# Gate and up projections as Strassen block products, a separate down projection through DRAM, and a merge in 512-column products

## The chip, the cores and the metric

The kernel runs on one core of a Trainium2 chip. The metric is the device time of one execution in microseconds; lower is better. PE below is the matrix engine, DVE, ACT and POOL are the vector, scalar and GpSimd engines, and SP issues most of the DMAs.

## The reference

One layer for a sequence of 1024 rows of width 1024, in float32. The change touches the lines after the two mixers (y_a, y_b), cut here to what matters:

```python
x = x + (g_a * y_a + g_b * y_b) @ w_out            # merge, w_out 1024 x 1024
h = rmsnorm(x, norm_ffn_g)
x = x + (silu(h @ w_ffn_gate) * (h @ w_ffn_up)) @ w_ffn_down   # D_FF = 2816
return rmsnorm(x, norm_final_g)
```

## The kernel before

Every float32 operand is split into a rounded part and the rest (`split`, L156: a cast to the short type `fp32r` on ACT, then a subtraction on DVE), and every product is three products of such parts: high by high, high by low, low by high (`mm3`, L145, products in L152 to L154). So a weight block costs a DMA, a cast `wh` (L161) and a subtraction `wl` (L164) before PE can use it. The class `Weights` (L75) holds a list of all weight blocks in the order of use, loads them into two raw buffers with DMAs of SP (L93) and splits them into three pairs of buffers `wh`, `wl`; `next` gives one block and prepares the ones behind it (`ahead`). Each engine does its instructions in the order in which the program wrote them, so the order of the calls is the order of each queue.

The stages at the end of the program are these. `up_b` (L1136) makes y_b, multiplies it by its gate, adds the other half and writes the merged activations `mhi`, `mlo` (64 groups of three 512-column products, the last `mlo` on POOL). `load_x1` (L1179) brings x into SBUF by four 1 MB DMAs on the ACT queue, in front of the casts of `up_b`. `merge` (L1184) multiplies by w_out: four column groups of 256, two halves of the inner dimension, eight row tiles, four blocks, three products each (L1199 to L1201), 768 products in all; the sum goes onto x1 in SBUF (L1206), the squares are summed on ACT (L1208), `norm` scales rows on DVE and POOL (L204 to L207) and `turn` transposes them on PE and splits them back into `mhi`, `mlo` (L209 to L220). `ffn` (L1259) then goes over 22 column blocks f of 128: `gate_up(f)` (L1265) gives 96 products of 512 columns (for f = 0: 192 of 256, set between the last turns of the merge), Silu on ACT (L1281), a product on DVE (L1285) and a split into `shi`, `slo`; after every second f `down(c)` (L1320) does 96 products of 512 columns (L1331 to L1333) and adds them to x1 in SBUF (L1336). The last `down` also sums squares (L1342), scales rows and stores them (L1347).

Functions that the diff touches, as they were:

## Time and profile before

| what | us |
|---|---|
| median of 3 runs | 1673.09 (1671.81 to 1673.85) |
| the profiled execution: its own time | 1678.37 |
| its span in the trace | 1676.6 |
| PE busy in that span | 1626.2 (97%) |
| DVE, ACT, POOL busy | 857.9, 516.7, 382.1 |

The times are of whole executions. The span is what the trace of one execution covers, from its first to its last instruction; the execution itself took 1.8 us longer. Busy time of PE counts an instruction from its start to its modelled end; consecutive products overlap, so what one product costs is read from the distance of two starts, not from its duration.

### The profile page before, as it was taken

The page shows a single profiled execution, that of the slowest core. Times are in us where ns is not written, and L with a number is a line of the kernel's source. Part 1 is how long each engine was busy: PE and PEld are TensorE (multiplying, and loading weights), DVE is VectorE, ACT ScalarE, POOL GpSimd, SP SyncE. Part 2 cuts the span into 40 slices and gives each one's busy share as a digit, 9 for nine tenths or more (in the row PEclk, how much of TensorE's full clock was granted, in tenths as well). Part 3 has the DMA queues.
Part 4 walks back from the last instruction along what each step waited for, and adds up shares of the span by engine and source line. Part 5 has one row for each costly group of instructions (what it writes and reads, how often), then busy time and mean ns, then how long its engine had stood idle before and what let it go on. Part 6 is the DMA issues. An engine that isn't in the chain of part 4 may idle for free.

```text
span 1676.6 us, 22642 instructions
## 1 busy us (share of the span) xinstructions
PE 1626.2 (97%) x8612; PEld 1385.2 (83%) x8612; DVE 857.9 (51%) x1685; ACT 516.7 (31%) x1136; POOL 382.1 (23%) x438
## 2 busy tenths in 40 slices
PE   8989999999998999998999999999999999999996
PEld 7767888888886899997799988888888888888885
DVE  7268776511325899997923623324324334243245
ACT  5212324312210698996122321111111211211113
POOL 1027676300112455564502300000000000000004
PEclk9999999999999999999999999999999999999999
DMA  6333442374339612102722021111111211111112
GB/s 213 96 105 107 132 128 79 102 182 120 118 100 278 170 42 57 34 27 103 250 63 64 27 62 51 38 50 51 50 38 51 63 38 48 53 50 39 50 38 100
DMA packets 166785, 145.50 MB, mean 87 GB/s; under 512 B 17434, under 2 KB 142774, under 8 KB 166679
## 3 DMA queue, kind: packets, MB, share of 16 engines
q1 hardware_dynamic: 165591, 139.88, 28.2%
q10 hardware_dynamic: 1088, 4.19, 0.6%
q8 instruction: 68, 1.11, 0.3%
q14 instruction: 38, 0.31, 0.1%
HBM read 109.83 MB, written 32.11 MB: 85 GB/s over the span
## 4 chain that ended last, share of the span: by engine, by line
PE 84%; DVE 5%; DMA 4%; ACT 2%; issue 1%; SPq 1%; POOL 1%; POOLq 0%; ACTq 0%; DVEq 0%
PE a L152 16%; PE a L154 16%; PE a L153 16%; PE O L1059 3%; PE T L1041 3%; PE S L943 3%; PE b L1331 2%; PE b L1332 2%; PE b L1333 2%; PE c L1333 2%; PE c L1331 2%; PE c L1332 2%; PE a L1201 2%; PE a L1199 2%; PE a L1200 2%
## 5 line engine op out<-in xcount | busy, mean ns | idle before, releaser
L152 PE MATMUL a<-mhi,wh 128*128 128x512 f32 (+1 forms) x736 | 280.0, 380 | 0.2 <-ACT mhi L219 0.2
L153 PE MATMUL a<-mlo,wh 128*128 128x512 f32 (+1 forms) x736 | 279.6, 380 | 0.3 <-DVE mlo L220 0.3
L154 PE MATMUL a<-mhi,wl 128*128 128x512 f32 (+1 forms) x736 | 279.6, 380 | 0.0
L164 DVE TENSOR_TENSOR wl<-wr,wh 128x1024 fp32r<-128x1024 f32 x108 | 142.0, 1316 | 254.9 <-ACT wh L161 242.0
L152 PE MATMUL a<-hhi,wh 128*128 128x512 f32 x448 | 185.0, 413 | 0.4 <-POOL wh L159 0.4
L154 PE MATMUL a<-hhi,wl 128*128 128x512 f32 x448 | 178.4, 398 | 2.2 <-DVE wl L164 2.2
L153 PE MATMUL a<-hlo,wh 128*128 128x512 f32 x448 | 178.5, 398 | 0.0
L206 POOL TENSOR_SCALAR x<-x,rstd 128x1024 f32<-128x1024 f32 (+1 forms) x4 | 8.2, 2038 | 707.6 <-DVE rstd L186 707.6
L153 PEld LDWEIGHTS a<-mlo,wh 128*128 128x128 f32 x736 | 138.4, 188 | 26.7 <-DVE mlo L220 0.5
L152 PEld LDWEIGHTS a<-mhi,wh 128*128 128x128 f32 x736 | 138.4, 188 | 26.7 <-ACT mhi L219 0.5
L154 PEld LDWEIGHTS a<-mhi,wl 128*128 128x128 f32 x736 | 138.4, 188 | 26.2
L161 ACT CAST wh<-wr 128x1024 fp32r<-128x1024 f32 x76 | 79.3, 1046 | 244.2 <-PE c L1333 173.4
L1014 POOL TENSOR_SCALAR P<-P,sum,gates 128x640 f32<-128x640 f32 (+3 forms) x192 | 125.4, 669 | 115.5 <-DVE sum L1008 64.4
L1043 DVE TENSOR_TENSOR PTl<-T,PTh 128x512 fp32r<-128x512 f32 (+3 forms) x200 | 104.0, 543 | 10.2 <-ACT PTh L1042 8.4
L152 PEld LDWEIGHTS a<-hhi,wh 128*128 128x128 f32 x448 | 85.7, 191 | 25.2 <-issue 6.2
L1336 DVE TENSOR_TENSOR x<-x,b 128x512 f32<-128x512 f32 x88 | 60.5, 687 | 87.3 <-PE b L1333 86.7
L154 PEld LDWEIGHTS a<-hhi,wl 128*128 128x128 f32 x448 | 85.5, 191 | 23.0 <-DVE wl L164 2.6
L153 PEld LDWEIGHTS a<-hlo,wh 128*128 128x128 f32 x448 | 85.9, 192 | 17.7
L994 ACT ACTIVATE P<-P,m 128x640 f32<-128x640 f32 (+7 forms) x128 | 95.8, 748 | 9.2 <-DVE m L978 9.2
L159 POOL TENSOR_SCALAR wh<-wr 128x1024 fp32r<-128x1024 f32 x34 | 36.9, 1085 | 259.4 <-PE a L153 149.8
L1042 ACT CAST PTh<-T 128x512 fp32r<-128x512 f32 (+3 forms) x200 | 88.7, 476 | 21.1 <-PE T L1041 20.4
L1281 ACT ACTIVATE sg<-a 128x512 f32<-128x512 f32 x44 | 26.3, 599 | 218.7 <-PE a L154 218.7
(353 smaller groups left out, 3389.0 us busy)
## 6 DMA issues: line engine op xcount, KB each, us to landing
wr<-in_w_in SPq DMA_DIRECT2D x28, 512.0 KB, 4.9
wr<-in_w_ffn_gate SPq DMA_DIRECT2D x22, 512.0 KB, 3.8
wr<-in_w_ffn_up SPq DMA_DIRECT2D x22, 512.0 KB, 4.0
wr<-in_w_ffn_down SPq DMA_DIRECT2D x22, 512.0 KB, 3.5
gd<-evf SPq DMA_DIRECT2D x32, 256.0 KB, 2.1
Q<-qd SPq DMA_DIRECT2D x64, 128.0 KB, 3.1
xt<-in_x SPq DMA_DIRECT2D x8, 512.0 KB, 5.7
sga<-gd SPq DMA_DIRECT2D x8, 512.0 KB, 5.0
```

Of the source, the lines that this page charges most:

```text
L152: mm(ps, a, c, start=start and k == 0, stop=False, skip_group_check=True)
L153: mm(ps, a, d, start=False, stop=False, skip_group_check=True)
L154: mm(ps, b, c, start=False, stop=stop and k == nk - 1, skip_group_check=True)
L161: nc.scalar.copy(hi, src)
L164: (nc.gpsimd if lo_eng == "pool" else nc.vector).tensor_tensor(lo, src, hi, op=OP.subtract)
L994: AC.activation(p[:, 0:nk], p[:, 0:nk], AF.Exp, bias=m[:, 0:1], scale=-1.0, accum_out=sm(0))
L1014: sc = lambda x, y, z: GP.tensor_scalar(x, x, a[:, y:y + 1], gate(z), op0=OP.mult, op1=OP.mult)
L1042: AC.copy(oh, t[:, 0:len(cc), :])
L1043: V.tensor_tensor(ol, t[:, 0:len(cc), :], oh, op=OP.subtract)
L1331: nc.tensor.matmul(ps, hi[:, t], wh[:, 0, col], start=f == 0, stop=False)
L1332: nc.tensor.matmul(ps, hi[:, t], wl[:, 0, col], start=False, stop=False)
L1333: nc.tensor.matmul(ps, lo[:, t], wh[:, 0, col], start=False, stop=f == 1)
```

## The change

Five things are done.

1. **Merge.** w_out is cut into units of two inner blocks by 512 columns (`unit`), and the products become 512 columns wide: 384 instead of 768. The first four row tiles use 8 units of 24 products; then the tiles 4 and 5, and 6 and 7, use 8 units each of 12 products, so w_out is read three times. x is loaded one tile at a time on the ACT queue (4 buffers `x1`), and after the norm a tile's x is stored to DRAM (`xd`), on the same queue.
2. **Turn.** For the tiles 4 to 7 `turn` also builds the sums of block rows that Strassen's scheme (in Winograd's form) needs, on DVE, POOL and ACT, in tiles with one buffer each, and splits five results.
3. **Gate and up.** 22 matrices (11 pairs of column blocks, gate and up in turn). Each is a 2 by 2 block product done with 7 block products of 12 products (512 columns), 84 in place of 96. The four sums of weight blocks are made on POOL (`sums`), the sums of results on DVE and POOL.
4. **Gated results** go to DRAM, 44 tiles `sd` of 256 KB, stored by SP.
5. **Down** is a phase of its own: 44 steps (two halves h of the rows, 22 f), 24 products each, all sums of a half in the eight PSUM banks; w_ffn_down is read twice, `sd` is read back, and x comes back from `xd` at f = 16. The squares and the scaling of tiles 0 to 3 run in the second half, those of tiles 4 to 7 at the end.

The order of the weight list is cut in two (`until`): w_ffn_down is loaded only from the end of the gate and up phase on. `Bacc` gets `dynamic_dma_scratch_size=1024`. The core of the diff (the removed `load_x1`, `merge` and `ffn` are printed above):

```diff
+    def load(self, n):
+        if n >= len(self.mats):
+            return
+        K, (name, j) = self.K, self.mats[n]
+        ts = []
+        for kh in range(2):
+            t = (K.W.raw if n % 2 else self.raw).tile([P, 4, 256], F32, name="wr", tag="wr")
+            K.nc.sync.dma_start(t, K.A[name][512 * kh:512 * kh + 512, 256 * j:256 * j + 256]
+                                .rearrange("(k p) c -> p k c", p=P))
+            ts.append(t)
...
+    def pair(self, n, a, b, src):
+        W, sh = self.K.W, [P, 2, 4, P]
+        hi, lo = W.hl.tile(sh, FR, name="wh", tag="wh"), W.hl.tile(sh, FR, name="wl", tag="wl")
+        if src is not None and b is not None:
+            self.K.split(hi, lo, src, "act", "dve")
+        else:
+            A = self.r[n]
+            for x, t in enumerate(((1, 1), (1, 2)) if b is not None else ((2, 2),)):
+                self.K.split(hi[:, x], lo[:, x], A(*t), "act", "dve")
...
+        s = self.s[n] = self.pool.tile([P, 4, 4, P], F32, name="S", tag="S", bufs=1)
+        o = lambda i: s[:, i]
+        GP.tensor_tensor(o(1), A(2, 1), A(2, 2), op=OP.add)
+        GP.tensor_tensor(o(0), o(1), A(1, 1), op=OP.subtract)
+        GP.tensor_tensor(o(2), A(1, 1), A(2, 1), op=OP.subtract)
+        GP.tensor_tensor(o(3), A(1, 2), o(0), op=OP.subtract)
...
+    def out(self, n, i, h, t):
+        K, (name, j) = self.K, self.mats[n]
+        if name == "w_ffn_gate":
+            K.nc.scalar.activation(t, t, AF.Silu)
+            self.gates[j, i, h] = t
+        else:
+            K.nc.gpsimd.tensor_tensor(t, t, self.gates.pop((j, i, h)), op=OP.mult)
+            K.nc.sync.dma_start(self.sd[2 * j + i][h], t)
...
+    def early(self):
+        self.sums(0)
+        self.p1(0)
+        self.p1(1)
+        self.p2(0)
+        self.p2(1)
...
+    def rest(self, n, early):
+        K, last = self.K, n + 1 == len(self.mats)
+        V, AC, GP = K.nc.vector, K.nc.scalar, K.nc.gpsimd
+        y = K.bank("b")
+        self.product(n, 6, y)
+        u2 = self.p.pop(n)
+        V.tensor_tensor(u2, u2, y, op=OP.add)
+        if not early:
+            self.p2(n)
+            self.t4(n)
+            self.load(n + 2)
+        z = K.bank("a")
+        self.product(n, 5, z)
+        p5 = self.tile("p5")
+        AC.copy(p5, z)
+        if n:
+            self.t1(n + 1)
+        v = K.bank("b")
+        self.product(n, 7, v)
+        u3 = self.tile("u3")
+        V.tensor_tensor(u3, u2, v, op=OP.add)
+        GP.tensor_tensor(p5, u3, p5, op=OP.add)
+        self.out(n, 1, 1, p5)
+        self.product(n, 3, z, first=False)
+        V.tensor_tensor(u2, u2, z, op=OP.add)
+        self.out(n, 0, 1, u2)
+        if last:
+            self.after()
+        self.t2(n + 1)
+        c = K.bank("c")
+        self.product(n, 4, c)
+        V.tensor_tensor(u3, u3, c, op=OP.add)
+        self.out(n, 1, 0, u3)
+    def run(self, after):
+        self.after = after
+        self.t2(0)
+        for n in range(len(self.mats)):
+            self.t3(n)
+            self.sums(n + 1)
+            if n < 2:
+                self.t4(n)
+                self.load(n + 2)
+            else:
+                self.p1(n)
+            self.rest(n, n < 2)
...
     def up_b(self, pool, m_):
...
-        self.load_x1(x1)
...
+        def load(tt):
+            x1[tt] = pool.tile([P, D], F32, name="x1", tag="x1", bufs=4)
+            nc.scalar.dma_start(x1[tt], self.A["x"][P * tt:P * tt + P, :])
...
+        def norm(tt):
+            xns[tt] = self.norm(pool, x1[tt], g, "xn", "dve", 2)
+            nc.scalar.dma_start(xd[tt], x1.pop(tt))
...
+            v = lambda n: pool.tile([P, 4, P], F32, name=n, tag=n, bufs=1)
+            t1, t2, t3, t4, b22 = (v(n) for n in ("t1", "t2", "t3", "t4", "b22"))
+            V.tensor_tensor(t1, pb, first(0, 0), op=OP.subtract)
+            AC.copy(b22, pc)
+            GP.tensor_tensor(t1, t1, first(1, 0), op=OP.subtract)
+            V.tensor_tensor(t3, b22, pb, op=OP.subtract)
+            GP.tensor_tensor(t2, b22, t1, op=OP.subtract)
+            GP.tensor_tensor(t4, first(0, 1), t2, op=OP.subtract)
+            GP.tensor_tensor(t4, t4, first(1, 1), op=OP.add)
+            for x, hi, lo in ((b22, m[0][:, 4:8, at], m[1][:, 4:8, at]),
+                              (t3, td[1][0][:, :, c], td[1][1][:, :, c]),
+                              (t1, m[0][:, 0:4, at], m[1][:, 0:4, at]),
+                              (t2, td[0][0][:, :, c], td[0][1][:, :, c]),
+                              (t4, td[2][0][:, :, c], td[2][1][:, :, c])):
+                self.split(hi, lo, x, "act", "dve")
+        unit = lambda u, q: self.W.next("w_out", 256 * u, 2, 512 * q, 512, ("act", "dve"))
+        for tt in range(4):
+            load(tt)
+        for q in range(2):
+            banks = [self.bank("a") for _ in range(4)]
+            for u in range(4):
+                w = unit(u, q)
+                for tt in range(4):
+                    part(w, u, tt, banks[tt])
+                    if u == 3:
+                        add(tt, q, banks[tt])
+                        if q and tt < 2:
+                            norm(tt)
+        load(4)
+        load(5)
+        for first in (4, 6):
+            for q in range(2):
+                banks = [self.bank("a") for _ in range(2)]
+                for u in range(4):
+                    w = unit(u, q)
+                    last = first == 6 and q == 1
+                    if last and u >= 2:
+                        if u == 2:
+                            ffn.load(1)
+                        ffn.t1(u - 2)
+                    for i in range(2):
+                        tt = first + i
+                        part(w, u, tt, banks[i])
+                        if u == 3:
+                            add(tt, q, banks[i])
+                            if q:
+                                norm(tt)
+                    if first == 4 and q == 0:
+                        turn(u)
+                        if u < 2:
+                            norm(u + 2)
+                            load(u + 6)
+                    if first == 6 and q == 0 and u % 2:
+                        turn(4 + u // 2)
+                    if first == 6 and q == 0 and u == 0:
+                        ffn.load(0)
+        ffn.early()
+        turn(6)
+        turn(7)
...
+                t = pool.tile([P, 512], F32, name="sr", tag="sr", bufs=4)
+                self.nc.sync.dma_start(t, sd[f][h])
...
+        for n, (h, f) in enumerate(order):
             if f == 0:
+                banks = [[self.bank("a" if tt < 2 else "bc"[c]) for c in range(2)] for tt in range(4)]
+            split(n + 2)
+            load(n + 4)
+            hi, lo = parts[n]
+            wh, wl = self.W.next("w_ffn_down", P * f, 1, 0, D, ("act", "dve"))
+            if f == 16:
+                for tt in range(4 * h, 4 * h + 4):
+                    x1[tt] = pool.tile([P, D], F32, name="x1f", tag="x1f", bufs=8)
+                    nc.sync.dma_start(x1[tt], xd[tt])
...
+                ss, one = (pool.tile([P, k], F32, name=f"ssf{k}", tag=f"ssf{k}", bufs=4) for k in (2, 1))
+                added(4 + tt, banks[tt], ss)
+                V.tensor_reduce(one, ss, axis=mybir.AxisListType.X, op=OP.add)
+                r = self.rstd(pool, one)
+                if tt < 3:
+                    scaled(4 + tt, slice(0, D), r, "pool" if tt == 1 else "dve")
+                else:
+                    scaled(7, slice(512, D), r, "pool")
+                    scaled(7, slice(0, 512), r, "dve")
...
+        def after():
+            W.until(None)
+            W.ahead(2, 4)
+            loads[3](1)
+        ffn.run(after)
+        for p in (ffn.late, fp, rp, tp, mp):
+            p.release()
+        pool = self.pool("dn")
+        self.down(pool, loads, xd)
...
```

The order of the engines' queues changes at three places that matter below. In the rows a name before the arrow is written, those behind it are read; a number behind a name tells buffers of that name apart; "waits" names the engine or the DMA queue that the instruction waits for.

ACT, in the merge between the products of tiles 0 to 3 and those of tiles 4 and 5. Before, at the same place (the last column group), the queue held squares, rstd, turns and casts of weights, and no DMA:

```order
L1208 ACTIVATE scr_8657,ssq0_8653<-x10_8248 128x256 [waits Activation_49]
L178 ACT_TABLE_LOAD
L178 ACTIVATE rstd_9411<-ss2_9409,eps_103 128x2 [waits DVE_49]
L1208 ACTIVATE scr_8657,ssq1_8654<-x11_8249 128x256 [waits DVE_49,Activation_49]
L1208 ACTIVATE scr_8657,ssq1_8654<-x11_8249 128x256 [waits Activation_49]
L178 ACTIVATE rstd_9452<-ss2_9450,eps_103 128x2 [waits DVE_49]
L219 CAST mhi_8246<-b_9512 128x4x128 [waits PE_49]
L219 CAST mhi_8246<-c_9519 128x4x128 [waits PE_49]
L161 CAST wh_9526<-wr_9322 128x1024 [waits DMAHW7_49,Pool_49]
```

Now:

```order
L1385 DMA xd0_8692<-x1_8706 128x1024
L376 ACTIVATE xn_8968,ss_8967<-x1_8708 128x1024 [waits DVE_49]
L360 ACTIVATE rstd_8970<-ss_8967,eps_103 128x1 [waits Activation_49]
L1385 DMA xd1_8693<-x1_8708 128x1024
L1369 DMA x1_8992<-in_x 128x1024 [waits DMAHW1_49]
L1369 DMA x1_8994<-in_x 128x1024 [waits DMAHW2_49,DVE_49]
L343 CAST wh_8998<-wr_8910 128x1024 [waits DMAHW7_49,PE_49]
```

The store of a tile's x, the load of the next tile into the same buffer and the cast of the next unit of w_out now stand one behind the other in ACT's queue.

ACT, at the end of the merge, the turns of the tiles 6 and 7 and what follows. Before, two turns were two casts each, with products of `gate_up(0)` on PE between them:

```order
L219 CAST mhi_8246<-b_9717 128x4x128 [waits PE_49]
L219 CAST mhi_8246<-c_9724 128x4x128 [waits PE_49]
L1281 ACT_TABLE_LOAD
L1281 ACTIVATE sg_9755<-a_9667 128x512 [waits PE_49]
L219 CAST mhi_8246<-b_9757 128x4x128 [waits PE_49]
L219 CAST mhi_8246<-c_9764 128x4x128 [waits PE_49]
```

Now:

```order
L343 CAST T0h_8642<-t2_9575 128x4x128 [waits Pool_49]
L343 CAST T2h_8646<-t4_9577 128x4x128 [waits Pool_49]
L1402 COPY b22_9610<-c_9597 128x512 [waits DVE_49,PE_49]
L343 CAST mhi_8246<-b22_9610 128x4x128 [waits Activation_49]
L343 CAST T1h_8644<-t3_9608 128x4x128 [waits DVE_49]
L343 CAST mhi_8246<-t1_9606 128x4x128 [waits Pool_49]
L343 CAST T0h_8642<-t2_9607 128x4x128 [waits Pool_49]
L343 CAST T2h_8646<-t4_9609 128x4x128 [waits Pool_49]
L343 CAST wh_9635<-S_9500 128x1024
```

The second turn's copy waits for the first turn's last results on DVE, and the cast of the weight sums S that the next product needs stands behind both turns.

SP, at the passage to the down phase. Before, the loads of w_ffn_down stood between those of the next gate and up blocks:

```order
L93 DMA wr_11671<-in_w_ffn_gate 128x8x128 [waits DMAHW5_49,DVE_49]
L93 DMA wr_11705<-in_w_ffn_up 128x8x128 [waits DMAHW6_49,DVE_49]
L93 DMA wr_11739<-in_w_ffn_gate 128x8x128 [waits DMAHW7_49,DVE_49]
L93 DMA wr_11875<-in_w_ffn_up 128x8x128 [waits DMAHW0_49,DVE_49]
L93 DMA wr_11935<-in_w_ffn_down 128x1024 [waits DMAHW1_49,DVE_49]
```

Now:

```order
L235 DMA sd211_8691<-p5_12426 128x512 [waits DMAHW7_49,Pool_49]
L235 DMA sd201_8689<-p1_12378 128x512 [waits DMAHW0_49,Pool_49]
L94 DMA wr_12461<-in_w_ffn_down 128x1024 [waits DMAHW1_49,Activation_49]
L94 DMA wr_12467<-in_w_ffn_down 128x1024 [waits DMAHW2_49,DVE_49]
L94 DMA wr_12473<-in_w_ffn_down 128x1024 [waits DMAHW3_49,DMAHW1_49,DVE_49]
L94 DMA wr_12475<-in_w_ffn_down 128x1024 [waits DMAHW4_49,DMAHW2_49,DVE_49]
L1469 DMA sr_12477<-sd00_8648 128x512 [waits DMAHW5_49]
```

The load of the first gated tile (`sr`) stands behind two stores that wait for POOL and behind two weight loads that wait for a split on DVE.

## Rows read from the trace of the kernel before

**Rows 1.** the page, part 1 (busy time) and the first line of part 4 (the chain)

```profile
PE 1626.2 (97%) x8612; PEld 1385.2 (83%) x8612; DVE 857.9 (51%) x1685; ACT 516.7 (31%) x1136; POOL 382.1 (23%) x438
...
PE 84%; DVE 5%; DMA 4%; ACT 2%; issue 1%; SPq 1%; POOL 1%; POOLq 0%; ACTq 0%; DVEq 0%
```

**Rows 2.** timeline of PE in a gate and up block: start, us, engine, line, output<-inputs

```profile
960.10 0.39 PE L152 MATMUL a<-mhi,wh 128*128 128x512 f32 x1
...
981.18 0.39 PE L152 MATMUL a<-mhi,wh 128*128 128x512 f32 x1
```

**Rows 3.** timeline of PE in a down block

```profile
1002.27 0.39 PE L1331 MATMUL b<-wh,shi 128*128 128x512 f32 x1
...
1008.57 0.40 PE L1331 MATMUL c<-wh,shi 128*128 128x512 f32 x1
```

**Rows 4.** timeline of PE in the merge's first products

```profile
833.52 0.28 PE L1199 MATMUL a<-wh,mhi 128*128 128x256 f32 x1
...
835.92 0.28 PE L1201 MATMUL a<-wh,mlo 128*128 128x256 f32 x1
```

**Rows 5.** timelines of ACT and PE in up_b; in brackets the wait and its releaser

```profile
785.27 4.67 ACTq L1181 DMA_DIRECT2D x<-in_x  x1
...
796.82 1.99 ACT L161 CAST wh<-wr 128x1024 fp32r<-128x1024 f32 x2 [10.53 <-DMA x<-in_x]
...
799.99 0.47 PE L152 MATMUL a<-oh,wh 128*128 128x512 f32 x1 [2.06 <-DVE sgb L1157]
```

**Rows 6.** groups by line and shape, 1050 to 1680 us: busy us, mean ns, waits

```profile
L161 ACT CAST wh<-wr 128x1024 fp32r<-128x1024 f32 x54 | 56.5, 1047 | 156.1 <-PE c L1333 156.1
...
L164 DVE TENSOR_TENSOR wl<-wr,wh 128x1024 fp32r<-128x1024 f32 x54 | 66.1, 1224 | 196.9 <-ACT wh L161 196.9
...
L164 DVE TENSOR_TENSOR slo<-sg,shi 128x512 fp32r<-128x512 f32 x36 | 24.9, 693 | 24.7 <-ACT shi L161 24.7
...
L1342 ACT ACTIVATE scr<-x 128x1024 f32<-128x1024 f32 x6 | 6.4, 1061 | 13.9 <-DVE x L1336 13.7
```

**Rows 7.** groups by line and shape, 780 to 960 us (merge)

```profile
L164 POOL TENSOR_TENSOR mlo<-sgb,mhi 128x512 fp32r<-128x512 f32 x16 | 24.4, 1526 | 30.7 <-DVE mhi L163 16.3 <-issue 14.4
...
L1158 DVE TENSOR_TENSOR sgb<-sgb,pab 128x512 f32<-128x512 f32 x16 | 19.5, 1221 | 0.6
...
L204 DVE SCALAR_TENSOR_TENSOR xn<-x,rstd,gffn 128x1024 f32<-128x1024 f32 x4 | 5.1, 1285 | 0.4
...
L219 ACT CAST mhi<-c 128x512 fp32r<-128x512 f32 x8 | 4.7, 591 | 0.0
...
L215 PE MATMUL b<-cst,xn 128*128 128x128 f32 x32 | 4.8, 273 | 1.7 <-DVE mlo L220 1.7
```

**Rows 8.** timeline of SP, first DMA of the merge

```profile
842.02 0.33 SPq L169 DMA_DIRECT2D gffn<-in_norm_ffn_g  x1
```

**Rows 9.** DMA issues: output<-input, queue, count, KB each, us to landing

```profile
wr<-in_w_out SPq DMA_DIRECT2D x8, 512.0 KB, 5.0
...
wr<-in_w_ffn_down SPq DMA_DIRECT2D x22, 512.0 KB, 3.5
...
out<-x SPq DMA_DIRECT2D x7, 512.0 KB, 2.6
```

**Rows 10.** timeline of PE after a wait early in the program

```profile
52.70 0.27 PE L417 MATMUL b<-cst,prm 96*128 96x96 f32 x1 [2.44 <-issue]
...
58.02 0.63 PE L152 MATMUL a<-hhi,wh 128*128 128x512 f32 x1
...
60.58 0.63 PE L152 MATMUL a<-hhi,wh 128*128 128x512 f32 x1
```

**Rows 11.** stretch 58 to 60 us: us, busy by engine (count), PEclk, DMA share, GB/s

```profile
58.00:60.00 2.00, 2.00 (x6) 1.59 (x5) 0.00 (x0) 0.00 (x0) 0.00 (x0) 0.50 0.03 8
```

**Rows 12.** timelines of PE and POOL at the end

```profile
1663.50 0.40 PE L1333 MATMUL c<-wh,slo 128*128 128x512 f32 x1
...
1671.05 1.57 POOL L207 TENSOR_TENSOR x<-x,gfin 128x512 f32<-128x512 f32 x1
```

More of the change, by code (lines that the diff above doesn't have):

```diff
@@ L84, in __init__ @@
         self.loaded, self.done = {}, {}
+        self.limit = None
         self.raw, self.hl = K.pool("wraw", 2), K.pool("whl", 3)
@@ L88, in load @@
         K = self.K
-        while self.nl < min(n, len(self.order)):
+        while self.nl < self.upto(n):
             name, r0, nk, c0, nc_, _ = self.order[self.nl]
@@ L97, in split @@
     def split(self, n):
-        while self.ns < min(n, len(self.order)):
+        while self.ns < self.upto(n):
             self.load(self.ns + 1)
@@ L105, in split, with upto, until @@
             self.ns += 1
+    def upto(self, n):
+        return min(n, len(self.order) if self.limit is None else self.limit)
+    def until(self, name):
+        if self.order is not None:
+            self.limit = None if name is None else [u[0] for u in self.order].index(name)
     def ahead(self, s, n):
@@ L1133, in attention, with up_b @@
             f(*a)
-    def up_b(self, pool, m_, x1):
+    def up_b(self, pool, m_):
         nc, V = self.nc, self.nc.vector
@@ new lines, in down_loads, with load, split @@
+    def down_loads(self, pool, sd):
+        order, raw, parts = [(h, f) for h in range(2) for f in range(NF)], [], []
+        def load(n):
+            while len(raw) < min(n, len(order)):
+                h, f = order[len(raw)]
+                t = pool.tile([P, 512], F32, name="sr", tag="sr", bufs=4)
+                self.nc.sync.dma_start(t, sd[f][h])
+                raw.append(t)
+        def split(n):
+            load(n)
+            while len(parts) < min(n, len(order)):
+                hi, lo = (pool.tile([P, 512], FR, name=x, tag=x, bufs=3) for x in ("shi", "slo"))
+                self.split(hi, lo, raw[len(parts)], "act", "dve")
+                parts.append((hi, lo))
+        return order, parts, load, split
@@ new lines, in down, with square, scaled, added @@
+    def down(self, pool, loads, xd):
+        nc, V, AC, mm = self.nc, self.nc.vector, self.nc.scalar, self.nc.tensor.matmul
+        gf = self.broadcast_row(pool, "gfin", self.A["norm_final_g"])
+        order, parts, load, split = loads
+        x1 = {}
+        def square(x, ss):
+            scr = pool.tile([P, D], F32, name="scr", tag="scr", bufs=1)
+            AC.activation(scr[:, 0:512] if x.shape[1] == 512 else scr, x, AF.Square, accum_out=ss)
+        def scaled(tt, c, r, eng):
+            x = x1[tt][:, c]
+            self.scaled(x, x, r, gf[:, c], eng)
+            nc.sync.dma_start(self.out[P * tt:P * tt + P, c], x)
+        def added(tt, banks, ss):
+            for c in range(2):
+                x = x1[tt][:, 512 * c:512 * c + 512]
+                V.tensor_tensor(x, x, banks[c], op=OP.add)
+                if ss is not None:
+                    square(x, ss[:, c:c + 1])
+        for n, (h, f) in enumerate(order):
+            if f == 0:
+                banks = [[self.bank("a" if tt < 2 else "bc"[c]) for c in range(2)] for tt in range(4)]
[7 more added lines that the diff above has]
+                    nc.sync.dma_start(x1[tt], xd[tt])
+            for tt in range(4):
+                t = slice(P * tt, P * tt + P)
+                for c in range(2):
+                    ps, col = banks[tt][c], slice(512 * c, 512 * c + 512)
+                    mm(ps, hi[:, t], wh[:, 0, col], start=f == 0, stop=False)
+                    mm(ps, hi[:, t], wl[:, 0, col], start=False, stop=False)
+                    mm(ps, lo[:, t], wh[:, 0, col], start=False, stop=f == NF - 1)
+                if f < NF - 1:
+                    continue
+                if h == 0:
+                    added(tt, banks[tt], None)
+                    continue
+                ss, one = (pool.tile([P, k], F32, name=f"ssf{k}", tag=f"ssf{k}", bufs=4) for k in (2, 1))
[4 more added lines that the diff above has]
+                    scaled(4 + tt, slice(0, D), r, "pool" if tt == 1 else "dve")
+                else:
+                    scaled(7, slice(512, D), r, "pool")
+                    scaled(7, slice(0, 512), r, "dve")
+            if h and 2 <= f < 10 and f % 2 == 0:
+                one = pool.tile([P, 1], F32, name="ssf1", tag="ssf1", bufs=4)
+                square(x1[f // 2 - 1], one)
+                scaled(f // 2 - 1, slice(0, D), self.rstd(pool, one), "dve")
```

279 lines of the change are left out of this document (92 added, 187 removed).

## The prediction

> **What bounds the kernel now.** I read the page first: PE is busy for 97% of the span and makes up 84% of the chain of waits [rows 1]. Then I read the timeline of PE for the distance of two starts, since a busy time of 0.39 us says little where products overlap. In a gate and up block 93 products lie between 960.10 and 981.18, so one takes 0.2267 us [rows 2]. In a down block 27 products take 6.30 us, 0.2333 each [rows 3]. The 256-column products of the merge take 2.40/20 = 0.120 [rows 4], so two of them cost 0.240, hardly more than one of 512 columns. With no waits, then, products times distance is the time; what the change saves on PE counts in full, and so does every wait that it puts in front of PE. The other engines have room: DVE 51%, ACT 31%, POOL 23% [rows 1].
>
> **The sum is made against the profiled span, 1676.6 us.** The median of the runs is 3.5 us below it, and I take that off at the end. About 0.2% (3.3 us) is what a measurement of this kernel can tell from no change.
>
> **What goes.** Gate and up now take 2016 products of 512 columns and 192 of 256: 2016 x 0.2267 + 192 x 0.120 = 480.1. Afterwards 22 x 84 = 1848 at 0.2267 are 418.9: **-61.1**. The merge goes from 768 x 0.120 = 92.2 to 384 x 0.2333 = 89.6: **-2.6**. Down keeps 1056 products. In `up_b` the casts stood 10.53 us behind the loads of x on ACT's queue, and PE waited 2.06 for it [rows 5]; these loads are gone from there: **-2.0**. Together -65.7.
>
> First the row, then a rule on it. The products of gate and up follow each other at 0.2267 us [rows 2], and nothing in the new code shortens that. The Trainium skill (page "TensorE: Matmul & The Clock Gate", section "Back-to-back issue gap") gives a sustained 131 ns for products of this width. By that the 264 products fewer would be worth about 35 us, not 60, as an estimate. The trace doesn't bear it out, and the sum goes by the row.
>
> **What the Winograd phase needs beside PE.** One matrix is 84 x 0.2267 = 19.0 us of PE. Its seven blocks are 3.5 casts of 1.05 and 3.5 subtractions of 1.22 us [rows 6], 3.7 on ACT and 4.3 on DVE; the sums of results add four steps of 0.69 on DVE, and POOL has four sums of weights and up to four steps on results, at 1.53 [rows 7] 12.2 us. All this fits under 19 us, so I cost it at nothing in the steady state. The cover is thinnest for the pair (6,5), whose sums come from POOL and whose split stands behind the results on DVE; by the order it is done some 1.8 us early.
>
> **What comes: waits of PE.** A unit of two tiles is 12 products, 2.8 us; a unit's weights cost 1.05 + 1.22 = 2.27 us after they have landed.
> - *Start of the merge.* The pools of the merge come free when the last `mlo` of `up_b` is done on POOL. Before, the first DMA that needs them went out at 842.02 [rows 8], 8.5 us after PE began the merge, with no harm. Now the loads of x need it and stand ahead of a cast on ACT. DVE is 2.06 less late, so 6.4 + 0.5 for the issues + 2.27, against 5.6 of the first unit: 3.6 (0 to 7).
> - *Tiles 4 and 5.* ACT's queue holds store of x, load into the same buffer, cast of the next unit. A store of this size landed in 2.6 us [rows 9]. With two casts of a turn (2 x 0.59 [rows 7]), a square 1.06 [rows 6], about 1.0 for rstd (estimate), 2.6, and 2.27, a unit is 8.1 apart, against 3.7 of products and transposes: 4.4, for two units; the next two, still catching up, 1.5 each (estimate). 11.9 together (2 to 14).
> - *Raw buffers.* Two buffers, 5.0 to land [rows 9] + 2.27 = 7.3 against 5.6 for two units: 1.7.
> - *The unit behind the norms of tiles 4 and 5.* Add 0.69, square 1.06, rstd 1.5 (estimate), cast 1.05, two scalings 2 x 1.29 on DVE [rows 7], subtraction 1.22: 8.1 less the 2.8 of one unit: 5.3 (0 to 6).
> - *Turns of 4 and 5.* DVE 0.69, four POOL steps 4 x 1.53, a cast 0.59 and the next weights 2.27 stand in a row, 9.65, and one unit of 2.8 covers it: 6.85, twice: 13.7 (5 to 15).
> - *First Winograd products.* The result of the first product is copied on ACT behind both norms: 3 (0 to 4.4).
> - *Turns of 6 and 7.* Their tiles have one buffer and DVE takes them in order, so the second starts when the first has ended: 2 x (0.69 + 6.1 + 0.59 + 0.69) = 16.1, then the cast and subtraction of the first sums, 2.27, some of it alongside. PE has nothing else: 18 (14 to 19). Before, two turns were two casts each beside products.
> - *Between the first two matrices:* 0.7.
> - *Passage to down.* SP issues the last stores, which wait for POOL, then four loads of weights, of which the third and fourth wait for splits, and only then the first gated tile. 0.69 + 2 x 1.53 + 3.5 (load of w_ffn_down [rows 9]) + 1.05 + 2 x 1.22 + 2.6 + 1.3 (cast and subtraction of half the width) + 0.8 for issues = 15.4, less 2.8 of the last product: 12.6 (8 to 15).
> - *End.* Before, 13.1 us lay between the last start on PE, 1663.50 (POOL's last at 1671.05), and the end [rows 12]. Now four tiles are finished on DVE in a row, about 5.1 us each (two adds, rstd, scaling, a wait for the square) against 1.4 on PE: 4 x 5.1 - 3 x 1.4 + 3.1 for the last store = 19.3: 6.2 more (2 to 8).
>
> In all 76.7.
>
> **The clock.** After a wait of 2.44 us on PE, followed by small products, the distance from 58.02 to 60.58 is 0.427 a product [rows 10], at a granted clock of 0.50 [rows 11], the lower level. Ten such products in place of 0.232 cost 2 us. The new waits are longer, but several stand back to back; I take 4 (0 to 18, if nearly every wait were followed by such a stretch).
>
> Sum: -65.7 + 76.7 + 4 = +15.0, so a span of 1691.6 and a median of **1688**. Most of it is waiting at the seams, not in the long phases.
>
> **Rivals.**
> - *Forecast, 0.52:* 1676 to 1702 by the sum of these bounds taken against each other.
> - *A, the weights stay ahead (0.22), the faster side.* Three split buffers hold units in advance. If the casts of w_out run far enough ahead of the stores and loads on ACT's queue, the four waits inside the merge (11.9 + 1.7 + 5.3 + 13.7 = 32.6) and the clock's 4 go. Then -65.7 + 44.1 = -21.6: 1651.5. It decides at a split that is done one unit (2.8 us) earlier. For it: in the merge before, PE waited only 1.7 us at the transposes [rows 7]. Against: before, no DMA stood in ACT's queue there, and a unit was twice as long.
> - *B, the distance is 0.2333 in the Winograd phase as well (0.15).* The phase has more traffic of DMAs and more writers, like the down blocks [rows 3]. 1848 x 0.0066 = 12.2 more: 1700.
> - *C, DVE and POOL hold each other up (0.11).* In `up_b` a DVE addition with two inputs in SBUF took 1.221 beside POOL's `mlo` [rows 7], where one of the same size took 0.693 with POOL idle [rows 6]. In the new phase POOL works 12 of 19 us beside DVE's splits. If one POOL step of 1.53 falls before the split of pair (6,5) in each matrix, the 1.8 of slack, already thinned by DVE's longer steps, is gone, and 20 matrices cost 30 more: 1718. The Trainium skill (page "SBUF — State Buffer", section "Who interferes with whom") says that DVE with two SBUF inputs and POOL reading SBUF exclude each other for a whole instruction; by that, and by the trace, C is no mishap but a matter of slack.
>
> **How the numbers follow.** The likeliest is the forecast, 1688. The range must reach to A and B and part of C: 1650 to 1712. It leaves out nearly all of C and what of A is below 1650. Faster by more than 0.2% (below 1669.7) are A and a little of the forecast: 0.26. Within 0.2%: 0.07. Slower: 0.67.
>
> **What would show it.** Right: in the new trace a distance of 0.227 in gate and up; gaps of PE at the end of the merge (about 18 us before the first product of pair (6,5)), at the passage to down (about 12) and waits named after ACT's casts or DVE's subtractions in tiles 4 to 7. Wrong: no wait over 2 us in the merge (A), a distance of 0.233 (B), or a wait on DVE in every matrix (C). If the merge's waits sum to less than 15 us, the forecast falls.

## The result, and the profile after

The changed kernel took 1704.17 us (median of 4 runs, 1700.69 to 1707.91), the kernel before 1673.47 beside it: a ratio of 1.0175, 95% interval 1.0159 to 1.0191. It is slower by 30.7 us; the forecast was slower by some 15. The profiled execution took 1707.91 with a span of 1706.0, 3.7 above the median, as the one of before stood 4.9 above its own.

The page of the changed kernel, busy time, the granted clock in 40 slices, and the first line of the chain (before: [rows 1]):

```profile
PE 1586.6 (93%) x7868; PEld 1323.6 (78%) x7868; DVE 926.2 (54%) x1735; ACT 623.7 (37%) x1266; POOL 564.4 (33%) x581
...
PEclk9999999999999999999998779999999997999998
...
PE 78%; DVE 8%; DMA 4%; ACT 3%; POOL 2%; issue 2%; SPq 1%; ACTq 0%; POOLq 0%; DVEq 0%
```

PE does less work, and the time is longer. In the granted clock there is now a hole of three slices and another of one, and the last slice stands at 8, where every slice of before stood at 9. The mean clock fell from 0.990 to 0.966.

Who PE waited for (engine and line that waits, the releaser: us in total, times, longest):

```profile
PE a L1375 <- ACT wh L343: 25.3, 7, 5.8
PE b L212 <- ACT wh L343: 16.1, 1, 16.1
PE a L1519 <- issue: 13.6, 1, 13.6
PE a L1376 <- DVE wl L346: 8.0, 9, 2.0
...
PE a L212 <- ACT p L225: 3.7, 1, 3.7
```

L1375 to L1377 are the merge, L212 to L214 the Winograd products, L1519 to L1521 the down phase. Then the timeline of PE in the steady state, one matrix apart (it answers to [rows 2]), and the first products behind the longest wait:

```profile
1100.45 0.39 PE L212 MATMUL b<-T0h,wh 128*128 128x512 f32 x1
...
1119.49 0.39 PE L212 MATMUL b<-T0h,wh 128*128 128x512 f32 x1
...
1009.22 0.80 PE L212 MATMUL b<-T0h,wh 128*128 128x512 f32 x1 [16.11 <-ACT wh L343]
...
1011.50 0.63 PE L213 MATMUL b<-T0l,wh 128*128 128x512 f32 x1
1011.92 0.63 PE L214 MATMUL b<-T0h,wl 128*128 128x512 f32 x1
```

84 products take 19.04 us, 0.2267 each, exactly as before and as forecast. Behind the wait they are 0.42 apart. The stretches of the profile say why (length; busy us and count of PE, PEld, DVE, ACT and POOL; granted clock, DMA share, GB/s):

```profile
1000.00:1010.00 10.00, 0.78 (x2) 0.50 (x2) 9.61 (x9) 5.18 (x8) 6.04 (x4) 0.50 0.00 1
1010.00:1020.00 10.00, 9.96 (x33) 7.71 (x32) 2.85 (x4) 1.22 (x3) 5.41 (x4) 0.72 0.40 107
1030.00:1040.00 10.00, 10.00 (x46) 8.29 (x45) 6.59 (x8) 2.68 (x4) 8.99 (x7) 1.00 0.20 52
```

While PE waited the clock was granted at 0.50, the lower of its two levels, and it was still there when the products came: 33 products in 10 us instead of 46. From the start of the merge to the last product the clock fell ten times; these are the stretches in which it stood at 0.50, cut to tenths of a us:

```profile
841.50:844.80 3.30, 3.30 (x9) 2.59 (x8) 0.01 (x1) 0.00 (x0) 1.04 (x1) 0.50 1.03 413
889.30:892.60 3.30, 3.30 (x8) 2.62 (x9) 2.91 (x7) 0.97 (x3) 0.00 (x0) 0.50 0.55 155
906.40:909.70 3.30, 3.30 (x10) 2.53 (x9) 2.47 (x4) 0.15 (x1) 0.00 (x0) 0.50 0.54 165
930.30:937.00 6.70, 5.71 (x15) 4.54 (x16) 2.07 (x2) 0.00 (x0) 0.00 (x0) 0.50 0.66 205
943.90:950.60 6.70, 4.16 (x9) 2.98 (x10) 4.71 (x5) 2.51 (x3) 0.43 (x1) 0.50 0.25 90
957.60:967.70 10.10, 4.61 (x10) 3.34 (x11) 8.32 (x5) 2.51 (x3) 9.42 (x6) 0.50 0.18 56
984.90:988.20 3.30, 3.30 (x10) 2.53 (x9) 0.33 (x1) 0.82 (x1) 0.00 (x0) 0.50 0.05 21
998.50:1015.50 17.00, 6.24 (x14) 4.51 (x15) 13.48 (x13) 6.61 (x10) 10.49 (x8) 0.50 0.11 31
1425.20:1438.70 13.50, 3.48 (x8) 2.77 (x9) 3.74 (x4) 2.71 (x3) 1.27 (x1) 0.50 0.37 113
1445.70:1449.00 3.30, 3.30 (x9) 2.58 (x8) 3.02 (x4) 1.75 (x3) 0.00 (x0) 0.50 0.22 50
```

**Where the time went.** From the timeline of PE I took, for each product, the distance to the next start less the wait shown with it. What is over 0.26 us counts as slow, and its excess is what it has over 0.2285; the first row takes the usual distances, 0.2267 and, in the merge, 0.228. Sums in us, against what the prediction had for the same place:

| place | forecast | measured |
|---|---|---|
| products of gate, up and merge | -63.7 | -65.7 |
| `up_b` | -2.0 | -0.2 |
| wait, start of the merge | 3.6 | 2.8 |
| waits, tiles 4 and 5 (x on ACT's queue) | 11.9 | 10.7 |
| waits, raw buffers and small ones | 1.7 | 1.8 |
| wait, unit behind the norms of 4 and 5 | 5.3 | 4.9 |
| waits, units behind the turns of 4 and 5 | 13.7 | 13.9 |
| wait, first Winograd products | 3.0 | 3.7 |
| wait, turns of 6 and 7; next matrix | 18.7 | 16.7 |
| waits, passage to down | 12.6 | 15.4 |
| end, longer by | 6.2 | 6.0 |
| slow products, merge to down | 4 | 24.9 |
| before's own waits there, not counted | 0 | -3.3 |
| start of `up_b` earlier | 0 | -1.8 |
| sum | 15.0 | 29.8 (span: 29.4) |

One row is far off: the slow products.

### The profile page after: what moved, and what is told of

Read it like the earlier page. It is cut to its first block, busy times and chain, and to the rows that moved or that the text cites. A ratio compares the mean times of both kernels' runs of the same rounds, so it can differ in the third digit from the quotient of the medians.

```text
span 1706.0 us, 22111 instructions
## 1 busy us (share of the span) xinstructions
PE 1586.6 (93%) x7868; PEld 1323.6 (78%) x7868; DVE 926.2 (54%) x1735; ACT 623.7 (37%) x1266; POOL 564.4 (33%) x581
## 4 chain that ended last, share of the span: by engine, by line
PE 78%; DVE 8%; DMA 4%; ACT 3%; POOL 2%; issue 2%; SPq 1%; ACTq 0%; POOLq 0%; DVEq 0%
PE a L334 7%; PE a L336 7%; PE a L335 7%; PE a L212 5%; PE a L213 5%; PE a L214 5%; PE O L1241 3%; PE T L1223 3%; PE S L1125 3%; PE b L214 2%; PE b L212 2%; PE b L213 2%; PE a L1521 2%; PE a L1519 2%; PE a L1520 2%
## 5 line engine op out<-in xcount | busy, mean ns | idle before, releaser
L346 DVE TENSOR_TENSOR wl<-wr,wh 128x1024 fp32r<-128x1024 f32 (+1 forms) x170 | 186.2, 1109 | 139.9 <-ACT wh L343 126.9
L343 ACT CAST wh<-wr 128x1024 fp32r<-128x1024 f32 (+1 forms) x138 | 113.4, 842 | 186.8 <-DMA wr<-in_w_out 42.0
L212 PE MATMUL a<-mhi,wh 128*128 128x512 f32 x352 | 138.0, 392 | 3.7 <-ACT p L225 3.7
L213 PE MATMUL a<-mlo,wh 128*128 128x512 f32 x352 | 137.8, 391 | 0.0
L214 PE MATMUL a<-mhi,wl 128*128 128x512 f32 x352 | 137.5, 391 | 0.0
L336 PEld LDWEIGHTS a<-hhi,wl 128*128 128x128 f32 x448 | 85.4, 191 | 22.9 <-DVE wl L346 2.6
L346 DVE TENSOR_TENSOR slo<-sr,shi 128x512 fp32r<-128x512 f32 x44 | 30.4, 691 | 133.3 <-ACT shi L343 133.3
L1160 DVE CUSTOM_DVE_ANT_0 P<-S,B 128x640 f32<-128x640 f32 (+7 forms) x128 | 89.5, 700 | 4.3 <-PE S L1125 2.1
L1223 PE MATMUL T<-cst,P 128*128 128x128 f32 x592 | 87.3, 274 | 3.7 <-DVE PTl L1225 3.1
L343 ACT CAST shi<-sr 128x512 fp32r<-128x512 f32 x44 | 27.3, 620 | 170.0 <-PE c L1520 154.4
L1519 PE MATMUL a<-wh,shi 128*128 128x512 f32 x176 | 71.0, 403 | 15.4 <-issue 13.6
```

The lines of the kernel that those rows point to most:

```text
L212: mm(ps, wh[:, k], bh[:, k], start=first and k == 0, stop=False, skip_group_check=True)
L213: mm(ps, wh[:, k], bl[:, k], start=False, stop=False, skip_group_check=True)
L214: mm(ps, wl[:, k], bh[:, k], start=False, stop=k == 3, skip_group_check=True)
L336: mm(ps, b, c, start=False, stop=stop and k == nk - 1, skip_group_check=True)
L343: nc.scalar.copy(hi, src)
L346: (nc.gpsimd if lo_eng == "pool" else nc.vector).tensor_tensor(lo, src, hi, op=OP.subtract)
```

## The experiments

In every run the ratio is to the kernel before, run beside it. The start of `up_b` lies between 777.8 and 783.9 us in these profiles (784.8 before) though nothing ahead of it differs, so stages are compared from there on: 923.1 us for the changed kernel, 891.8 before.

### e1_warm: products of zeros in the waits

```diff
+        def warm(n):
+            b = self.bank("c")
+            for _ in range(n):
+                mm(b, zero[:, 0:P], zero, start=True, stop=True)
...
+        fill = {(4, 0, 0): 14, (4, 0, 1): 9, (4, 0, 2): 15, (6, 0, 0): 18, (6, 0, 2): 24, (6, 1, 0): 30}
...
+                    if (first, q, u) in fill:
+                        warm(fill[first, q, u])
...
+        warm(66)
```

> Nothing is removed; products of zeros with zeros into an unused PSUM bank are put in front of the waits of PE: 10 before the second unit of the merge, 14, 9, 15, 18, 24 and 30 before units of tiles 4 to 7, 15 before the second early product, 66 behind the last turn, 58 before the down phase (some 60 us of products in waits of some 70). The results are the same. Theory 'clock': in the changed kernel about 125 products beside waits are 0.2 us too slow, 26 us in all from the merge to the down phase, because the granted clock falls to 0.50 while PE waits; with PE busy through the waits the clock stays and about 20 of the 26 us go: 1684 (1678 to 1690), granted clock near 0.99, the waits named before shorter by what the zeros fill. Rival 'operands': the first products after a wait are slow because their operands and PE's queue have to start again; then the zeros change nothing: 1704, within 4. Rival 'in the way': the zeros are still running when the operands come, 1705 to 1712.

Measured: 1696.98 us, ratio 1.0119 (1.0100 to 1.0138), mean clock 0.981. Slow products from the merge to the down phase cost 11.3 us instead of 24.9. The time lies between the range of "clock" and that of "operands". Where zeros filled the wait, the slow stretch went; where they ran in the wrong place or a wait was left, it stayed: three stretches are left of ten. Zeros and waits together were 77.1 us long where waits alone had been 69.8. The timeline of PE and the stretch around the longest wait:

```profile
983.69 15.23 PE L1373 MATMUL c<-warm 128*128 128x512 f32 x66
1000.27 0.50 PE L212 MATMUL b<-T0h,wh 128*128 128x512 f32 x1 [1.34 <-ACT wh L344]
1000.61 0.40 PE L213 MATMUL b<-T0l,wh 128*128 128x512 f32 x1
...
1002.87 0.61 PE L212 MATMUL b<-T0h,wh 128*128 128x512 f32 x1
...
985.00:995.00 10.00, 10.00 (x46) 8.28 (x45) 9.86 (x9) 4.22 (x8) 7.59 (x5) 1.00 0.15 49
995.00:1005.00 10.00, 7.82 (x30) 5.72 (x29) 8.15 (x8) 3.66 (x5) 5.39 (x5) 0.89 0.03 4
```

The clock stayed at 1.00 through the stretch in which it had stood at 0.50, and the first products came 0.23 to 0.40 us apart, waits taken off, where they had been 0.42 to 0.67. The zeros ended too early, though: waits of 1.34 and 0.83 us are left behind them, and at 1002.87 the clock fell after all, for 3.4 us, and the slow products there cost 1.7. So "clock" is right in kind: the operands arrive as late as before, and where the clock stays up the slowness goes. Of the expected 20 us, 13.6 were got and 7.3 paid back to overruns. From the start of `up_b` to the end it gained 9.3; the 3.0 beyond the difference of these two lie outside this count, in transposes (1.1), `up_b` (0.5) and small amounts elsewhere.

### e2_passage: loads for the down phase issued earlier

```diff
         if not early:
...
+        if last:
+            self.after(0)        # W.until(None); W.ahead(0, 2); loads[2](4)
...
         self.out(n, 1, 1, p5)
+        if last:
+            self.after(1)        # loads[3](1); W.ahead(2, 4)
```

> Only the passage to the down phase is changed: the first two loads of w_ffn_down and the first four loads of gated tiles are issued in the middle of the last matrix, before the last stores that wait for POOL, and their splits before the last matrix's last two blocks. Theory 'order of SP's queue': the wait of 13.65 us before the first down product and the 1.74 behind it fall to under 2, and the 3.9 us of slow products behind them go as well: 1686 (1684 to 1690). If only the wait goes and the slow products stay: 1690. Rival 'landing': the gated tiles come late for another reason (their stores, the landing of 3.7 us each behind 1 MB of weights), the wait stays above 8: 1698 or more.

Measured: 1683.07 us, ratio 1.0043 (1.0028 to 1.0059). SP's queue and the first down product, in the changed kernel and then here:

```profile
1419.69 1.60 SPq L235 DMA_DIRECT2D sd<-p  x2
1421.38 7.80 SPq L94 DMA_DIRECT2D wr<-in_w_ffn_down  x4
1429.23 0.42 SPq L1469 DMA_DIRECT2D sr<-sd  x1
...
1435.22 0.77 PE L1519 MATMUL a<-wh,shi 128*128 128x512 f32 x1 [13.65 <-issue]
```

```profile
1407.72 0.84 SPq L94 DMA_DIRECT2D wr<-in_w_ffn_down  x2
1408.61 2.12 SPq L1471 DMA_DIRECT2D sr<-sd  x4
...
1417.20 0.40 PE L1521 MATMUL a<-wh,shi 128*128 128x512 f32 x1
```

Four loads of weights, two of them waiting for splits, had held the first gated tile back for 7.8 us. Issued in time, no wait is left, and no slow product either: the whole down phase has neither. Waits and slow products of the passage, 15.4 + 4.0 = 19.4, went together. The time is 0.9 us below the expected range; from the start of `up_b` 22.9 us were gained, 2.1 of them in `up_b`, which the edit doesn't touch.

### e3_turns: the end of the merge in another order

```diff
-        ffn.early()
-        turn(6)
-        turn(7)
+        ffn.sums(0)
+        ffn.p1(0)
+        ffn.p1(1)
+        ffn.t2(0)
+        turn(6)
+        ffn.p2(0)
+        turn(7)
+        ffn.p2(1)
```

`t2(0)`, the split of the first pair (6,5), stood at the start of `run` before.

> Only the order at the end of the merge is changed: the split of the first pair (6,5) stands before the last two turns, and the turns of tiles 6 and 7 stand between the early products instead of behind them. No operation is added or removed. Theory 'chain in a row': the two chains of 8.0 us start about 7 us earlier and the 2 us cast behind them is gone from the chain; the wait of 16.1 falls to 6 to 8, the time by 8 to 12 with the clock: 1694 (1690 to 1697). Rival 'engines full': DVE and POOL are the bound of that stretch whatever the order, the wait moves to another product: 1702 to 1706.

Measured: 1692.95 us, ratio 1.0103 (1.0088 to 1.0118). Before the first product of pair 6 there are now two waits:

```profile
993.89 0.80 PE L212 MATMUL b<-T0h,wh 128*128 128x512 f32 x1 [8.54 <-ACT T0h L342]
997.69 0.80 PE L213 MATMUL b<-T0l,wh 128*128 128x512 f32 x1 [3.00 <-DVE T0l L345]
```

11.5 us instead of 16.1, and the stretch from the first Winograd product to pair 6 fell from 34.6 to 24.4, as "chain in a row" had it. The wait itself is longer than the expected 6 to 8. In this trace DVE's subtractions beside POOL's steps take 1.5 to 1.8 us in both turns, and 0.68 where no step of POOL runs beside them; that this is the whole reason isn't shown, for in e9, with POOL out of the turns, the waits here are 5.9 us, against 5.6 in e8.

### e4_loads: the loads of x two units later on ACT's queue

```diff
-        load(4)
-        load(5)
...
-                            load(u + 6)
+                        for tt in {1: (4, 5), 3: (6, 7)}.get(u, ()):
+                            load(tt)
```

> Only the place of the loads of x for tiles 4 to 7 on ACT's queue is changed: each stands two units later, behind the casts that it stood in front of, when the store into the same buffer's place in DRAM has long landed. Theory 'ACT's queue': the waits before the first three units of tiles 4 and 5 (3.14 + 0.76, 1.89 + 0.76, 3.35 + 0.76 = 10.7) fall to under 3 together, and about 6 us of slow products with them: 1690 (1687 to 1697). Rival 'weights late anyway': two raw buffers of w_out at 5.2 us each to land hold the units back, the waits are renamed to the DMA or to the subtraction and add up to the same: 1700 to 1705.

Measured: 1693.09 us, ratio 1.0104 (1.0085 to 1.0123). ACT in the changed kernel, a load that waits for a store's landing and the cast behind it, and then the same cast here:

```profile
894.92 0.33 ACTq L1369 DMA_DIRECT2D x<-in_x  x1
895.30 1.04 ACT L343 CAST wh<-wr 128x1024 fp32r<-128x1024 f32 x1 [5.00 <-DMA xd<-x]
```

```profile
883.26 1.05 ACT L343 CAST wh<-wr 128x1024 fp32r<-128x1024 f32 x1
```

The waits of these three units fell from 10.7 to 4.5 us, not under 3: one of 2.6 is left, for DVE's subtraction, which stands behind a scaling and two additions there. The 6 us of slow products did not go with them: from the merge to the down phase 24.2 are left of 24.9. In these units one stretch is left of two, but others grew, the one at the first Winograd products from 1.7 to 2.5.

### e5_tail: the last three steps tile by tile

```diff
+            late.append((f, hi, lo, wh, wl))
+            if h and NF - 3 <= f < NF - 1:
+                continue
+            now, late = late, []
             for tt in range(4):
...
+                for f, hi, lo, wh, wl in now:
```

> Only the end of the down phase is changed: the last three steps of the second half are done tile by tile (18 products for tile 4, then for tile 5, and so on) instead of step by step, so that the tiles are finished 4.2 us apart, where DVE needs about 5.1 for each. Theory 'four tiles in a row on DVE': 19.1 us from the last product's start to the end become about 11, 1696 (1694 to 1698) against 1704. Rival 'last store': what ends the run is one store's landing and POOL's scaling whatever the order, 1702 to 1705. Rival 'weights': the third step's weights and gated tile now have to be split before the first of the three begins, PE waits there, and half of the gain is given back: 1699 to 1702.

Measured: 1690.79 us, ratio 1.0082 (1.0059 to 1.0104). The last product starts at 1675.26 of 1685.8, so 10.5 us are left behind it where there had been 19.1: 8.6 gained, as forecast, for one more wait of 0.8. The rest of the 13 us lies in stages that the edit doesn't touch (by the profiles 2.9 in the waits of tiles 4 and 5, 1.9 in `up_b` and 1.2 in slow products, all of which differ from one execution to the next), and isn't its gain.

### e6_sum and e7_best: the edits together

e6_sum is e2, e3 and e4. e7_best adds e5, a second buffer for two of the turn's tiles, the loads of x at the merge's start behind the second unit's cast, and

```diff
-            GP.tensor_tensor(t1, t1, first(1, 0), op=OP.subtract)
+            V.tensor_tensor(t1, t1, first(1, 0), op=OP.subtract)
...
+            self.held += [(0, td[0][0][:, :, c], td[0][1][:, :, c], t2), (2, td[2][0][:, :, c], td[2][1][:, :, c], t4)]
...
                     w = unit(u, q)
+                    release()              # splits what is held
...
+                    if first == 4 and q and u == 3:
+                        self.W.ahead(2, 4)
```

> The three edits of the runs on the passage to down, the order of the last turns and the place of the loads of x, all together. Theory 'the waits are independent': the gains add, -22 -12 -12 of a median of 1704 (taken as ratios to the kernel before), about 1658, a ratio of 0.990 to the kernel before (0.987 to 0.993). Rival 'the clock shared': part of what each gained was one clock stretch counted twice, 1664 to 1672, a ratio of 0.994 to 0.999.

> All of the edits, and four more for the waits that are left in the merge: the last two splits of a turn of tiles 4 to 7 stand behind the next unit's cast; the first of a turn's four steps on POOL is done on DVE and two of the turn's tiles have two buffers; the loads of x at the merge's start stand behind the cast of the second unit; at the last unit before the norms one more unit is split ahead. Theory 'waits and clock': beyond the sum of the three and the end (1658 - 8) the waits 5.6, 5.8 + 2.0, 3.4 + 1.4 and 2.0 + 0.8 go by about two thirds and their slow stretches with them: 1634 (1626 to 1642), a ratio of about 0.976. Rival 'engines full': what is split earlier delays other splits on ACT and DVE, the merge stays where it is: 1648 to 1655.

Measured: 1669.19, ratio 0.9946 (0.9929 to 0.9963), and 1650.38, ratio 0.9835 (0.9817 to 0.9852). The ratios of e2, e3 and e4 had promised 46 us of gain against the changed kernel; e6 has 38 by its ratio, which falls in the rival's range, though its interval reaches to the edge of the other. The traces don't bear the rival's reason out: by waits and slow products the three gained 19.5, 9.9 and 6.9 us, together 36.3, and e6 gained 35.0. The difference between the medians lies outside the stages edited, or in the error of four comparisons of some 3 us each; which of the two is open. Counted from the start of `up_b`, the profiled executions give 43.4 against 38.0, and 2.5 of these 5.4 lie in `up_b` itself, which none of the edits touches. e7 lies in the range of its rival, "engines full": of the 21.0 us of waits that were named, two thirds were to go, and the 28.4 of the whole merge became 20.9, since units behind the turns stayed late.

### e8_order and e9_dve: one more unit ahead, and POOL out of the turns

```diff
+                        self.W.ahead(2, 4)
                         turn(4 + u // 2)
```

(e8, with the splits of the last turns in the order of use and a second buffer for `t1`), and in e9 also

```diff
-            GP.tensor_tensor(t2, b22, t1, op=OP.subtract)
-            GP.tensor_tensor(t4, first(0, 1), t2, op=OP.subtract)
-            GP.tensor_tensor(t4, t4, first(1, 1), op=OP.add)
+            V.tensor_tensor(t2, b22, t1, op=OP.subtract)
+            V.tensor_tensor(t4, first(0, 1), t2, op=OP.subtract)
+            V.tensor_tensor(t4, t4, first(1, 1), op=OP.add)
```

> The kernel with all edits and the four more, and two orders in it changed: one more unit of w_out is split ahead before the turns of tiles 4 and 5, and the splits of the last two turns stand in the order in which the products need them (pair 6 first, its sums before those of the other pairs), behind the first half of the last turn. No operation is added or removed. In the kernel before it 20.9 us of waits were left in the merge and 8.0 at the turns of 6 and 7, 9.0 of it before the first product of pair 6. Theory 'waits are a matter of the order on ACT and DVE': 5 of the 9.0 and 5 to 7 of the 7.6 at the two units behind the turns go, with 3 of slow products: 1636 (1632 to 1642), a ratio of about 0.975. Rival 'DVE full': DVE has all of these splits to do in that stretch, waits only change their names: 1647 to 1653.

> The last kernel (1643, ratio 0.9795) with one change: the three steps of a turn of tiles 4 to 7 that are left on POOL are done on DVE. In that kernel's trace DVE's subtractions beside POOL's steps take 1.75 us instead of 0.69, each about a POOL step (1.59) apart. Theory 'one of the two at a time': without POOL's steps the subtractions of a turn fall back to 0.69, DVE's work of a turn from about 10.5 to 7.6 us though it has three steps more, and the wait of 4.5 + 3.7 before the third last unit falls by 3 to 5: 1638 (1634 to 1642). Rival 'DVE full': DVE is the longer queue there in any case and three more steps cost more than they save: 1644 to 1650, with subtractions that stay over 1 us.

Measured: 1643.44, ratio 0.9795 (0.9775 to 0.9815), and 1640.14, ratio 0.9789 (0.9773 to 0.9806); as times the two can't be told apart. e8 lies just above its expected range and below the rival's: the waits before pair 6 fell from 9.0 to 5.6 us, but in the merge, where 5 to 7 more were to go, 20.8 are left of 20.9. In the traces e8 and e9 can be told apart. DVE and POOL in the turn of tile 5, in e8:

```profile
937.74 1.47 DVE L347 TENSOR_TENSOR mlo<-b,mhi 128x512 fp32r<-128x512 f32 x1
939.14 1.75 DVE L347 TENSOR_TENSOR T1l<-t,T1h 128x512 fp32r<-128x512 f32 x1
940.81 1.75 DVE L347 TENSOR_TENSOR mlo<-t,mhi 128x512 fp32r<-128x512 f32 x1
```

```profile
938.75 1.59 POOL L1407 TENSOR_TENSOR t<-mhi,t 128x512 f32<-128x512 f32 x1
940.42 1.59 POOL L1408 TENSOR_TENSOR t<-t,mlo 128x512 f32<-128x512 f32 x1
```

and DVE in e9:

```profile
936.99 0.68 DVE L347 TENSOR_TENSOR mlo<-b,mhi 128x512 fp32r<-128x512 f32 x1
937.59 0.68 DVE L347 TENSOR_TENSOR T1l<-t,T1h 128x512 fp32r<-128x512 f32 x1
```

Beside POOL each subtraction ends 1.67 us after the one before, the pace of POOL's steps; without POOL they are 0.6 apart. The Trainium skill (page "SBUF — State Buffer", section "Who interferes with whom") has DVE with two SBUF inputs and POOL reading SBUF exclude each other; the rows here agree, 1.75 against 0.68. The wait before the last unit but one fell from 8.2 to 2.0 us, 2.3 came back two units earlier, and the merge as a whole went from 122.7 to 118.7; from the first Winograd product to pair 6, where DVE now does POOL's steps too, 18.6 became 19.8.

### e10_zeros: products of zeros in the three longest waits that e8 has left

```diff
+                    warm({(6, 0, 2): 12, (6, 1, 2): 32}.get((first, q, u), 0))
...
         ffn.p2(1)
+        warm(20)
```

Here `warm(n)` makes 2n products of 256 columns.

> The last kernel (1643, ratio 0.9795) with products of zeros in front of the three places where it still waits over 3 us (3.3 before a unit behind the turn of tile 4, 8.2 before a unit behind that of tile 5, 5.6 before the first product of pair 6): 2.9, 7.5 and 4.7 us of them. The results are the same. Theory 'clock': the three stretches of 13, 11 and 11 slow products (2.96 + 2.59 + 2.58 us too long) shrink to the two or three slow starts that any wait has (0.3 to 0.5 each), and nothing else moves: 1637 (1634 to 1640). Rival 'in the way': a wait can't be met within a product, what the zeros overrun eats the gain: 1642 to 1646.

Measured: 1641.99, ratio 0.9796 (0.9782 to 0.9811): no gain. The three slow stretches all but went, as the clock theory had it, from 2.96, 2.59 and 2.58 us to 0.27, 0.15 and 0.37. But from the first Winograd product to pair 6 PE needed 2.0 us more (20.6 against 18.6), as "in the way" had it, and two other waits, of 1.7 and 2.5 us, now had slow products behind them (1.8 each). A wait is cheaper removed than filled.

## Why the prediction was right or wrong

The direction and the place were right, and the time lies in the range. The size was half of what came, and one step is the cause.

**Products.** Right. 0.2267 a product in the Winograd phase, so rival B (0.2333) is out, and 0.228 in the merge. The change saves what its arithmetic says, 66 us.

**Waits.** Right nearly term by term, 69.8 us of waits on PE against 70.5, and the places are the ones named. Rival A, weights that stay ahead of the stores and loads on ACT's queue, is out: the merge alone waited 34 us. The passage was 2.8 too low, 1.7 of it a second wait, for the next gated tile, that was left out. (The terms given for tiles 4 and 5 add up to 11.8, not 11.9.) e2, e3, e4 and e5 take single causes away, and the waits named go with them (e2) or shrink.

**The clock, the step that failed.** The prediction said "I take 4 (0 to 18, if nearly every wait were followed by such a stretch)", two stretches at the 2 us that [rows 10] gave. The price was nearly right (2.2 on average) and the count was wrong. From the merge to the down phase the clock fell ten times, and behind it stood 10 stretches of 8 to 14 slow products, counted from the first one behind the wait, that cost 1.7 to 3.3 us each, 21.9 of the 24.9; the rest are one or two slow products at a time, up to 0.4 us together. I had supposed that waits close together share one stretch, where nearly each had its own. Even the upper end was too low. e1 and e10 show the cause by keeping the waits and filling them, and the slow stretches go where they are filled; e2 shows that removing a wait removes its stretch.

**`up_b`.** The wait that was to go did go, and -2.2 is what this stage shows in the profiles in which the clock stayed up through it (46.4 to 46.6 us in e2, e5 and e10, against 48.7 before). In the profiled execution of the changed kernel the clock fell at 783.44, and 15 products from the start on were slow (3.5 us); it fell there in seven of the ten experiments' profiles as well, and not in the one of before. Why it falls one way or the other isn't settled.

**DVE and POOL (rival C).** Its mechanism is there, but not where I put it. In the steady state DVE's subtractions of weight sums took 1.46 us on average (1.21 to 2.24, from 1050 to 1415 us), where before one of this size took 1.22, and the slack held: apart from 0.54 us at its second matrix, PE waited for nothing in 22 matrices. In the turns three of the five subtractions took 1.75 us. The chain that I had put at some 8.1 us still took no more than 8.4 in each of the last two turns: its price for a POOL step, 1.53, had been read beside DVE's additions [rows 7], and the steps came 1.67 apart. That e3 and e7 gained less than expected for the same reason is not shown: e9 takes POOL out of the turns and gains 4.0 in the merge, but nothing before pair 6.

So the large expected gain is not lost in contention. It is given back as waiting at the seams, and the waiting costs a good third more than its own length, most of it through the clock.

## What to carry to other kernels

When a change saves work on an engine that was busy without a break, count every new wait that it puts in front of that engine, and add the price of the slow stretch behind it (here about 2 us at 10 of the 11 places with a wait of over 1.5 us), wait by wait. At the short ones it can go either way: a wait of 1.69 us before the same unit had such a stretch behind it in e10 and none in e8. Look at each queue for a load, a store or a split that stands ahead of something urgent only because it was written first: moving such things here, with some work handed from POOL to DVE and no operation removed, turned a kernel 1.75% slower than its predecessor into one 2.1% faster (e9). In the turns, work shared out to POOL beside DVE, both with two operands in SBUF, didn't run in parallel; what that costs is read from the duration of DVE's own instructions.

## What I had not expected of the hardware

Waits some 15 us apart were each followed by a stretch of their own at the lower clock. Products of zeros held the clock at 1.00 in the stretch shown, until the waits behind them. And DVE beside POOL came one after the other in the turns, 1.67 us a step, so that the engine with the shorter work (0.68) got the pace of the slower (1.59).
